# Bands and output projection of an encoder trunk: odd pairs' value products ahead of the scores, the last value splits in two steps, and the second half's normalising on VectorE

## The chip, the cores and the metric

The kernel runs on one core of a Trainium2 chip. The core has a matrix engine (TensorE, "PE" in the profile, with its weight loads listed apart as "PEld"), VectorE ("DVE"), ScalarE ("ACT"), GpSimd ("POOL") and a queue that issues most DMAs (SyncE, "SP"). Each engine works through its own instructions in order. The metric is the device time of one execution in microseconds (us); the median of some runs is compared.

## The reference

The reference is a trunk of two layers over 1024 tokens of width 1024, all in float32. Each layer computes

```python
h = rms_norm(x, g_attn[l]) * (1 + sc_a) + sh_a
proj = h @ w_in[l]
qa, ka, va, qb, kb, vb, qc, kc, vc = split_cols(proj, IN_SPLITS)
ya = neighborhood_attention(...)      # A: 4 heads, 2-D window with a relative bias
yb = sliding_window_attention(...)    # B: 6 heads on 2 key heads, |i-j| <= 128, sink logit
yc = axial_attention(...)             # C: 6 heads on 2 key heads, dense, rotary
ga, gb, gc = split_cols(g_group[l], GROUP_WIDTHS)
y = jnp.concatenate([rms_norm(ya, ga), rms_norm(yb, gb), rms_norm(yc, gc)], axis=-1)
x = x + gt_a * (y @ w_o[l])
h = rms_norm(x, g_ffn[l]) * (1 + sc_f) + sh_f
gate, up = split_cols(h @ w_gu[l], (FFN_HIDDEN, FFN_HIDDEN))
x = x + gt_f * ((jax.nn.silu(gate) * up) @ w_down[l])
```

A last RMS norm closes the trunk. What matters here: three groups of heads (widths 256, 384 and 384) give parts of `y`; each part is normalised over its own width, multiplied with a gain, and the whole goes through one output projection `w_o`.

## The kernel before, in words

**Layout.** Activations stand transposed: 128 features on the partitions, tokens along the free dimension. `y` has eight chunks of 128 features by 1024 tokens: chunks 0 and 1 are group A, 2 to 4 group B, 5 to 7 group C. Tokens are worked in two halves of 512 (`H`). To keep float32 accuracy on TensorE, an operand is split into a rounded high part and a low part (the rest), and a product is three matmuls: high x high, low x high, high x low (`mm3`, line 202).

**Attention as a stream of pairs.** Lines 1732 to 1744 write the work as a list of 64 pairs: six C heads, four A heads, six B heads, each with four pairs `p` = 0 to 3 of two query blocks (256 queries). The loop over turns `n` (line 1767) handles several pairs at once, each at another step. Pairs 0 to 23 are dense (C); pairs 24 to 63 are the bands (class `Band`, line 1560), whose queries see three key blocks each. In a turn of the bands (lines 1794 to 1814), for pair numbers around `n`, the steps are:

- `divide` of an older pair (VectorE reciprocal, then GpSimd scales the probabilities), `low` of pair n-1 (VectorE computes the low part of the transposed probabilities), `combine` of pair n-3 (VectorE adds the two halves of the value products into `y`; in the profile `y<-pv,cmb`);
- `scores` of pair n+4 (TensorE `sA` or `sB`, then VectorE adds the bias and takes the row's bound);
- `exps` of an older pair (ScalarE);
- `turn` of pair n: TensorE transposes the probabilities (`T`), ScalarE casts the middle blocks to the high part (`pt<-T`) and copies the edge blocks (`edge<-T`);
- `pv` of pair n-2: TensorE multiplies with the values into `pv`; then `fold` of the same pair: ScalarE copies one half of the partitions (`cmb<-pv`).

`fold` and `combine` do something only for odd pairs (line 1433 and 1442), because two pairs share one PSUM bank of 512 columns: the even pair opens a new `pv` tile in `products` (line 1413), the odd one fills its other half. The pool of these tiles has one bank (`bufs=4 - PS_T`, line 1361; `PS_T` is 3, the number of banks for `T`). So the products of an even pair wait until `combine` has read the bank for the pair before. Since pairs and turns have the same parity, even pairs are multiplied in even turns.

**What sets the order.** In the bands the instructions of TensorE, ScalarE and VectorE are pinned: `pin` (line 92) chains each to the one before it on its engine, so that these three run in the order of the program text. Instructions written while nothing is pinned are placed by a planner, which goes by data that is ready and by estimated costs, and can put them far ahead of their place in the text. That holds for what a turn does behind its `pin(..., False)` (line 1822): value splits, weight splits, output-projection rows, statistics.

**Norms.** When a group's pairs are done, `stats` (line 1865) sums squares over the partitions with one-column matmuls (`ps_st`) and takes the inverse root with a chain of small VectorE instructions (`inv_sqrt`; `isq` and `rstd` in the profile), all 1024 tokens at once. Eight turns after the group's end `norm_scale` (line 1684) follows: for each half, `spread` (line 449) makes four transposes that lay the 512 factors out over all partitions (`ps_r`), ScalarE copies them to `rb`, and one multiply for each chunk writes the normalised `y<-y,rb`. In the bands this is done for group C (three chunks) and A (two), both halves on GpSimd, one multiply a turn. Group B ends with the bands; it is normalised in the output projection, at `ki == 3` (line 1921), one half on VectorE and the other on GpSimd.

**Value splits.** `y_split` (line 1702) multiplies a chunk's half with the gain: ScalarE writes the high part, VectorE the low part. The first half's five normalised chunks (in the order `korder`: 5, 6, 7, 0, 1) go to a tile `yq`, which the profile calls `qk`: two are written in turns 55 and 59 (line 1837), three in the output projection at `ki == 0` (line 1916).

**Output projection.** Six of the eight output columns (`NK`) accumulate in PSUM over the chunks in the order `korder`, `ki` = 0 to 7; four of them (`NS`) start inside turns 61 to 64 (lines 1845 to 1848). The loop `for ki in range(5)` (line 1910) does the other columns and chunks, then columns 6 and 7, then `ki` = 5 to 7 with the split group B. The weights `w_o` come by DMA into two staging buffers and are split by ScalarE (`whi`) and VectorE (`wlo`). After that the second half is split for all chunks (line 1962) and projected.

Of the kernel before, what the change touches and what calls it, by code (L numbers as in the profile page):

```python
# [10 lines left out]
F32 = mybir.dt.float32  # L11
# [8 lines left out]
P = 128  # L20
D = 1024
S = 1024
KC = D // P
H = 512
# [61 lines left out]
def trunk(ctx: ExitStack, tc, A, C, out):  # L86
# [320 lines left out]
    def rstd_cols(ssqs, width, nt, sp_, psp, tag="mm", newton=False):  # L407

        ps = psp.tile([P, 512], F32, name="ps_st", tag=tag)
        for j in range(nt):  # L410
            for i, s in enumerate(ssqs):
                pe.matmul(
                    ps[:, j : j + 1],
                    s[:, j * P : (j + 1) * P],
                    ones,
                    start=(i == 0),
                    stop=(i == len(ssqs) - 1),
                )
        r = sp_.tile([P, 8], F32, name="rstd", tag="rstd", bufs=2)
        if newton:  # L420
            inv_sqrt(r[:, :nt], ps[:, :nt], width, sp_)
            return r
        act.activation(r[:, :nt], ps[:, :nt], AF.Sqrt, bias=epst, scale=1.0 / width)
        dve.reciprocal(r[:, :nt], r[:, :nt])
        return r
# [479 lines left out]
    for l in range(2):  # L905
# [775 lines left out]
            square(sq)  # L1681
            pool.tensor_tensor(out=ss[:, c], in0=ss[:, c], in1=sq, op=ALU.add)

        def norm_scale(chunks, r, psp, tag, engines):

            todo = []
            for half, eng in enumerate(engines):
                c = slice(half * H, (half + 1) * H)
                ps = spread(r, 4 * half, psp, tag=tag)
                rb = atp.tile([P, H], F32, name="rb", tag="rb", bufs=2)  # L1690
                act.copy(rb, ps)
                for n in chunks:
                    todo.append(
                        lambda eng=eng, n=n, c=c, rb=rb: eng.tensor_tensor(
                            out=y[:, n, c], in0=y[:, n, c], in1=rb, op=ALU.mult
                        )
                    )
            return todo

        korder = (5, 6, 7, 0, 1, 2, 3, 4)  # L1700

        def y_split(k, half, hi, lo):

            c = slice(half * H, (half + 1) * H)
            g = vec[:, 64 + k : 65 + k]
            act.activation(hi, y[:, k, c], AF.Copy, scale=g)
            dve.scalar_tensor_tensor(
                out=lo, in0=y[:, k, c], scalar=g, in1=f32(hi), op0=ALU.mult, op1=ALU.subtract
            )

# [44 lines left out]
            23: ((5, 6, 7), 384.0), 39: ((0, 1), 256.0), 63: ((2, 3, 4), 384.0),  # L1757
        }
        begins = {23: 0, 39: 24, 63: 40}
        later = {}  # L1760
        N = len(stream)
        pairs = {}
# [4 lines left out]
        for n in range(-AHEAD - 1, N + 3):  # L1767
# [26 lines left out]
            else:  # L1794
# [4 lines left out]
                if NC <= n - 3:  # L1799
                    pairs[n - 3].combine()  # L1800
                fresh = [pairs[m] for m in begin if m < made]
                for b in fresh:
                    b.scores()
                for b in scored:
                    b.exps()
                if n < N:
                    pairs[n].turn()
                if NC <= n - 2 < N:
                    pairs[n - 2].pv()
                    pairs[n - 2].fold()  # L1810
                elif n == NC:
                    for i in range(2):
                        pairs[n - 1].pv(i)
# [23 lines left out]
            if n in (55, 59):  # L1837
                ki = (n - 55) // 4
                y_split(korder[ki], 0, yq[:, ki, 0:H], yq[:, ki, H:S])
            if n in (59, 61):  # L1840
                w01.append(split_tile(wst.pop(0), 1, (atp, "pr", 6), dve))
            if n == 60:
# [9 lines left out]
            for end, (chunks, width) in norms.items():  # L1852
                if begins[end] <= m <= end and (m - begins[end]) % 8 == 7 and (n <= NC or m >= NC):
# [9 lines left out]
                    if m == end and end < N - 1:  # L1863

                        def stats(end=end, width=width, n=n, chunks=chunks):
                            r = rstd_cols([gss[end]], width, 8, atp, psT, tag="T", newton=True)

                            def scale():
                                todo = norm_scale(chunks, r, psT, "T", (pool, pool))
                                for i, what in enumerate(todo):  # L1870
                                    later.setdefault(n + 9 + i, []).append(what)

                            later.setdefault(n + 8, []).append(scale)

                        later.setdefault(n + 5, []).append(stats)
# [34 lines left out]
        for ki in range(5):  # L1910
            if ki < 2:
                o_rows(ki, w01[ki], range(NS, NK))
                w_ahead(3)
            else:
                o_rows(ki, w_next(), range(NK))
            if ki == 0:
                for i in range(2, 5):
                    y_split(korder[i], 0, yq[:, i, 0:H], yq[:, i, H:S])
            if ki == 2:
                r = rstd_cols([gss[N - 1]], norms[N - 1][1], 8, atp, psl, newton=True)  # L1920
            if ki == 3:
                for what in norm_scale(norms[N - 1][0], r, psl, "mm", (dve, pool)):
                    what()
                yb = [
                    atp.tile([P, 3, H], F32R, name="yb", tag="zA", bufs=2) for _ in range(2)
                ]
                for i in range(3):
                    y_split(2 + i, 0, yb[0][:, i, :], yb[1][:, i, :])
# [661 lines left out]
```

## Time and profile before

| what | value |
|---|---|
| median of 3 runs | 2369.87 us (2369.44 to 2372.74) |
| the profiled execution, its own time | 2368.57 us |
| its span, first to last instruction | 2366.8 us |
| granted TensorE clock, mean | 0.998 |
| busy: TensorE, VectorE, ScalarE, GpSimd | 2325.0, 1756.6, 1184.7, 775.7 us |
| bands of the first layer | about 364 to 464 us of the span |
| its output projection, first half | about 464 to 509 us |
| bands of the second layer | about 1521 to 1622 us |

How to read the lines in this document: an instruction is written as output `<-` inputs by the program's tile names, with buffer numbers left out, then partitions x elements and type. All lines carry "L49", the line of the helper that records every operation, so one goes by the tiles. In a listing in order of time the columns are start, duration (from the first start to the last end where equal neighbours are merged, `x` and their count) and the engine; in square brackets stands how long the engine had been idle and what ended that. In a list of waits the columns are the waiting engine and tile, what it waited for, the total in us, how many times, and the longest. Matmuls overlap, so the time that a group costs is read from its start to the next group's start.

### The profile page before, as it was taken

What the parts mean: (1) busy time and instruction counts of PE and PEld (TensorE: products, weight loads), DVE (VectorE), ACT (ScalarE), POOL (GpSimd) and SP (SyncE); (2) the same over time, 40 slices, a digit from 0 to 9 for tenths busy, and PEclk for the clock granted to TensorE, in tenths of its full rate; (3) what the DMA queues carried; (4) which work ended last, traced back from release to release, by engine and by line L of the source; (5) the groups of instructions that cost most, each with busy time, mean ns of one, the idle gap of its engine ahead of it and who ended that gap; (6) DMA issues with size and microseconds to landing.
All of it is one profiled execution on the core that took longest, in us unless ns stands there. A gap on an engine that the chain in (4) does not pass through costs nothing. (4 is left out here: it accounts for less than half of the span.)

```text
span 2366.8 us, 33472 instructions
## 1 busy us (share of the span) xinstructions
PE 2325.0 (98%) x11804; PEld 1959.9 (83%) x11804; DVE 1756.6 (74%) x2753; ACT 1184.7 (50%) x2261; POOL 775.7 (33%) x747
## 2 busy tenths in 40 slices
PE   9999999999999999999999999999999999999998
PEld 7888898888788888788888889988878888888886
DVE  6877998869867677595767789897796674537765
ACT  4423888845543333344633168896454434334443
POOL 1530447610344445100145124574005444430001
PEclk9999999999999999999999999999999999999999
DMA  8667416162434444775434861332634443239633
GB/s 280 182 207 227 127 27 192 44 217 94 138 130 165 156 138 151 217 245 175 155 100 133 247 186 28 92 103 94 218 98 132 154 150 103 98 106 299 209 120 112
DMA packets 307417, 358.02 MB, mean 151 GB/s; under 512 B 51996, under 2 KB 223868, under 8 KB 307248
## 3 DMA queue, kind: packets, MB, share of 16 engines
q1 hardware_dynamic: 290752, 346.26, 46.4%
q10 hardware_dynamic: 16128, 9.44, 1.5%
q8 instruction: 93, 1.52, 0.3%
q14 instruction: 76, 0.62, 0.1%
q0 software_dynamic: 368, 0.17, 0.0%
HBM read 270.84 MB, written 88.63 MB: 152 GB/s over the span
## 5 line engine op out<-in xcount | busy, mean ns | idle before, releaser
L49 PE MATMUL ps_d<-wpt 128*128 128x512 f32 x1848 | 423.8, 390 | 1.0 <-ACT wpt L49 0.7
L49 PEld LDWEIGHTS ps_d<-wpt 128*128 128x128 f32 x1848 | 345.7, 188 | 74.4 <-issue 3.0
L49 POOL TENSOR_SCALAR pr<-pr,rs 128x1024 f32<-128x1024 f32 (+2 forms) x248 | 190.3, 780 | 186.2 <-DVE rs L49 169.7
L49 POOL TENSOR_TENSOR sg<-sg,u 128x512 f32<-128x512 f32 x82 | 118.0, 1440 | 348.4 <-ACT sg L49 221.6
L49 PE MATMUL pv<-pt,vs 128*128 128x256 f32 x1088 | 173.9, 296 | 14.6 <-DVE y L49 13.3
L49 DVE TENSOR_TENSOR pt<-T,pt 128x512 fp32r<-128x512 f32 x272 | 177.4, 680 | 7.0 <-ACT pt L49 5.9
L49 ACT CAST wpt<-w 128x512 fp32r<-128x512 f32 x154 | 95.7, 621 | 173.5 <-PE ps_d L49 155.3
L49 DVE SCALAR_TENSOR_TENSOR acc<-wmt,condT,acc 128x512 f32<-128x512 f32 (+1 forms) x98 | 117.0, 1202 | 77.7 <-DMA wmt<-in_w_mod_dram 77.2
L49 ACT CAST pt<-T 128x512 fp32r<-128x512 f32 x272 | 151.5, 585 | 42.0 <-PE T L49 40.7
L49 ACT COPY u<-ps_w 128x512 f32<-128x512 f32 x128 | 75.1, 586 | 192.9 <-PE ps_w L49 192.9
L49 POOL TENSOR_TENSOR wpt<-ws,wpt 128x512 fp32r<-128x512 f32 x80 | 111.2, 1390 | 182.2 <-ACT wpt L49 137.2
L49 DVE TENSOR_TENSOR wpt<-w,wpt 128x512 fp32r<-128x512 f32 x154 | 108.9, 707 | 79.2 <-ACT wpt L49 76.9
L49 PEld LDWEIGHTS pv<-pt,vs 128*128 128x128 f32 x1088 | 141.0, 189 | 27.2 <-DVE y L49 25.2
L49 PE MATMUL T<-identr,pr 128*128 128x128 f32 x1176 | 160.1, 273 | 0.9 <-ACT edge L49 0.5
L49 PEld LDWEIGHTS T<-identr,pr 128*128 128x128 f32 x1176 | 137.7, 140 | 16.0 <-issue 1.4
L49 ACT CAST wpt<-ws 128x512 fp32r<-128x512 f32 x176 | 107.7, 622 | 52.9 <-issue 22.9
L49 DVE TENSOR_TENSOR wpt<-graw,wpt 128x512 fp32r<-128x512 f32 x154 | 109.8, 713 | 16.6 <-ACT wpt L49 16.4
L49 ACT CAST wpt<-graw 128x512 fp32r<-128x512 f32 x154 | 95.0, 617 | 52.7 <-DMA graw<-gpd 43.6
L49 DVE TENSOR_TENSOR wpt<-ws,wpt 128x512 fp32r<-128x512 f32 x96 | 82.7, 869 | 49.3 <-ACT wpt L49 49.1
L49 DVE TENSOR_TENSOR ws<-wr 128x512 f32<-128x512 f32 x88 | 81.2, 923 | 50.0 <-POOL wpt L49 46.6
L49 DVE TENSOR_REDUCE rs<-sC 128x1 f32<-128x1024 f32 x88 | 107.4, 1221 | 12.7 <-PE sC L49 11.4
L49 PE MATMUL ps_w<-ht3h,wpt 128*128 128x512 f32 x352 | 108.8, 390 | 2.4 <-ACT sg L49 2.4
(306 smaller groups left out, 5931.5 us busy)
## 6 DMA issues: line engine op xcount, KB each, us to landing
wr<-in_w_gu_dram SPq DMA_DIRECT2D x92, 512.0 KB, 4.2
gpd<-sg SPq DMA_DIRECT2D x154, 256.0 KB, 4.4
graw<-gpd SPq DMA_DIRECT2D x76, 512.0 KB, 3.5
w<-in_w_down_dram SPq DMA_DIRECT2D x110, 256.0 KB, 5.4
wmt<-in_w_mod_dram SPq DMA_DIRECT2D x48, 512.0 KB, 5.9
qk<-qkd SPq DMA_DIRECT2D x44, 512.0 KB, 7.2
wst<-in_w_o_dram SPq DMA_DIRECT2D x32, 512.0 KB, 4.4
wmt<-in_w_mod_dram SPq DMA_DIRECT2D x64, 256.0 KB, 3.9
```

Source lines behind the costliest of these rows:

```text
L49: ins = op(*args, **kwargs)
```

## The change

Three edits are made together.

1. In a turn of the bands, the value products `pv` of pair n-2 are issued ahead of the scores and the transposes if that pair is odd, and as before behind the transposes if it is even. `fold` stays behind the transposes in both cases.
2. `y_split` is taken apart: `y_high` issues ScalarE's high part and returns VectorE's low part as a function to be called later. The three splits that stood at `ki == 0` of the output projection are now issued in turns 62 to 64, the high part in one turn, the low part in the next (63 to 65), and both engines are pinned for them.
3. `norm_scale` takes a list of (half, engine). In the bands it is called for the first half alone, on GpSimd. The factors `r` of groups C and A are kept in a list `held`, and at `ki == 1` of the output projection the second half is spread and multiplied on VectorE. For this the tile `rstd` has three buffers instead of two where the chain of small instructions is used.

```diff
-        r = sp_.tile([P, 8], F32, name="rstd", tag="rstd", bufs=2)
+        r = sp_.tile([P, 8], F32, name="rstd", tag="rstd", bufs=3 if newton else 2)
...
-        def norm_scale(chunks, r, psp, tag, engines):
+        def norm_scale(chunks, r, psp, tag, halves):
 
             todo = []
-            for half, eng in enumerate(engines):
+            for half, eng in halves:
                 c = slice(half * H, (half + 1) * H)
                 ps = spread(r, 4 * half, psp, tag=tag)
                 rb = atp.tile([P, H], F32, name="rb", tag="rb", bufs=2)
...
-        def y_split(k, half, hi, lo):
+        def y_high(k, half, hi, lo):
 
             c = slice(half * H, (half + 1) * H)
             g = vec[:, 64 + k : 65 + k]
             act.activation(hi, y[:, k, c], AF.Copy, scale=g)
-            dve.scalar_tensor_tensor(
+            return lambda: dve.scalar_tensor_tensor(
                 out=lo, in0=y[:, k, c], scalar=g, in1=f32(hi), op0=ALU.mult, op1=ALU.subtract
             )
+
+        def y_split(k, half, hi, lo):
+            y_high(k, half, hi, lo)()
...
+        held, y_low = [], []
...
                 fresh = [pairs[m] for m in begin if m < made]
+                ready = pairs[n - 2] if NC <= n - 2 < N else None
+                if ready and ready.p % 2:
+                    ready.pv()
                 for b in fresh:
                     b.scores()
                 for b in scored:
                     b.exps()
                 if n < N:
                     pairs[n].turn()
-                if NC <= n - 2 < N:
-                    pairs[n - 2].pv()
-                    pairs[n - 2].fold()
+                if ready:
+                    if ready.p % 2 == 0:
+                        ready.pv()
+                    ready.fold()
                 elif n == NC:
...
+            if n >= 62:
+                pin((act, dve), True)
+                if y_low:
+                    y_low.pop()()
+                if n < 65:
+                    ki = n - 60
+                    y_low.append(y_high(korder[ki], 0, yq[:, ki, 0:H], yq[:, ki, H:S]))
+                pin((act, dve), False)
...
                             r = rstd_cols([gss[end]], width, 8, atp, psT, tag="T", newton=True)
 
+                            held.append((chunks, r))
+
                             def scale():
-                                todo = norm_scale(chunks, r, psT, "T", (pool, pool))
+                                todo = norm_scale(chunks, r, psT, "T", ((0, pool),))
...
-            if ki == 0:
-                for i in range(2, 5):
-                    y_split(korder[i], 0, yq[:, i, 0:H], yq[:, i, H:S])
+            if ki == 1:
+                for chunks, r in held:
+                    for what in norm_scale(chunks, r, psl, "mm", ((1, dve),)):
+                        what()
             if ki == 2:
                 r = rstd_cols([gss[N - 1]], norms[N - 1][1], 8, atp, psl, newton=True)
             if ki == 3:
-                for what in norm_scale(norms[N - 1][0], r, psl, "mm", (dve, pool)):
+                for what in norm_scale(norms[N - 1][0], r, psl, "mm", ((0, dve), (1, pool))):
                     what()
```

## The prediction

> **What bounds the kernel now.** I read the page first, then busy time by stretch, then the waits of the first layer's bands, and last the instructions in order of time in one head and in the stretch behind it.
>
> ```profile
> span 2366.8 us, 33472 instructions
> PE 2325.0 (98%) x11804; PEld 1959.9 (83%) x11804; DVE 1756.6 (74%) x2753; ACT 1184.7 (50%) x2261; POOL 775.7 (33%) x747
> ```
>
> TensorE is busy 98% of the span, so what can be won is mostly its idle 41.8 us, and whatever adds to it is lost. Stretches of the first layer (columns: length, then busy time and count of PE, PEld, DVE, ACT and POOL, granted clock, DMA):
>
> ```profile
> 394.99:453.60 58.61, 53.70 (x412) 50.63 (x412) 54.53 (x170) 55.90 (x158) 48.23 (x87) 1.00 0.21 62
> 453.60:464.44 10.84, 10.02 (x67) 8.15 (x66) 8.07 (x10) 7.64 (x18) 8.17 (x8) 1.00 0.30 101
> 464.44:489.00 24.56, 24.44 (x128) 20.34 (x127) 14.09 (x23) 10.85 (x15) 5.74 (x5) 1.00 0.40 128
> ```
>
> In the bands TensorE idles 4.9 of 58.6 us and ScalarE only 2.7. In the output projection TensorE idles 0.12 of 24.56: an instruction added to TensorE there costs its full time. The waits between 350 and 460 us:
>
> ```profile
> PEld pv L49 <- DVE y L49: 10.1, 15, 1.6
> PE pv L49 <- DVE y L49: 6.1, 10, 1.3
> ACT pt L49 <- PE T L49: 5.9, 11, 1.1
> ACT cmb L49 <- PE pv L49: 1.5, 3, 0.9
> DVE pr L49 <- POOL pr L49: 0.4, 1, 0.4
> ```
>
> TensorE's longest wait is the value products `pv` on the combine `y`. But ScalarE waits on TensorE's transposes `T` nearly as long, and that decides what the first edit does. Two pairs of turns, from all engines:
>
> ```profile
> 403.57 0.69 DVE L49 TENSOR_TENSOR y<-pv,cmb 64x512 f32<-64x512 f32 x1
> 404.32 0.74 PE L49 MATMUL pv<-pt,vs 128*128 128x256 f32 x4 [0.49 <-DVE y L49]
> 405.27 0.95 PE L49 MATMUL sB<-qk 128*128 128x384 f32 x4
> 406.06 0.82 PE L49 MATMUL T<-identr,pr 128*128 128x128 f32 x6
> 406.63 0.72 PE L49 MATMUL pv<-pt,vs 128*128 128x256 f32 x4
> 406.69 0.59 ACT L49 CAST pt<-T 128x512 fp32r<-128x512 f32 x1 [0.28 <-PE T L49]
> 407.18 0.38 ACT L49 COPY edge<-T 128x256 f32<-128x256 f32 x1
> 407.33 0.96 PE L49 MATMUL sB<-qk 128*128 128x384 f32 x4
> 407.67 0.58 ACT L49 COPY cmb<-pv 64x512 f32<-64x512 f32 x1
> 408.28 0.69 DVE L49 TENSOR_TENSOR y<-pv,cmb 64x512 f32<-64x512 f32 x1 [0.19 <-ACT cmb L49]
> 409.03 0.74 PE L49 MATMUL pv<-pt,vs 128*128 128x256 f32 x4
> 409.75 0.83 PE L49 MATMUL sB<-qk 128*128 128x384 f32 x4
> 410.42 0.71 PE L49 MATMUL T<-identr,pr 128*128 128x128 f32 x5
> 410.88 0.72 PE L49 MATMUL pv<-pt,vs 128*128 128x256 f32 x4
> 411.43 0.57 ACT L49 CAST pt<-T 128x512 fp32r<-128x512 f32 x1
> 411.80 0.83 PE L49 MATMUL sB<-qk 128*128 128x256 f32 x4
> 411.89 0.27 ACT L49 COPY edge<-T 128x128 f32<-128x128 f32 x1
> 412.19 0.58 ACT L49 COPY cmb<-pv 64x512 f32<-64x512 f32 x1
> 412.81 0.68 DVE L49 TENSOR_TENSOR y<-pv,cmb 64x512 f32<-64x512 f32 x1
> ```
>
> This is a closed loop. The one bank of `pv` is free when `y` has read it; then come the even pair's products (404.32), the next turn's scores `sB` (405.27), its transposes (406.06), ScalarE's cast of them (406.69), the edge copy, the fold `cmb` (407.67), and `y` again (408.28). From end of `y` to end of `y` it is 4.71 us here (404.26 to 408.97) and 4.52 in the second pair of turns (408.97 to 413.49).
>
> **The change, part by part.**
>
> *Odd pair's products first.* The odd pair's products (406.63 to 407.33, 0.70 us; 410.88 to 411.80, 0.92 us) move from behind the transposes of an odd turn to ahead of its scores, directly behind the even pair's. That puts them inside the loop, since TensorE works in order, and `cmb` stays behind the cast of the same turn's transposes. What was beside the loop is now on it. First pair of turns: the cast already waited for T, so it comes 0.70 later; against that `cmb` no longer waits for the products. It started 0.49 after the two-block edge copy, and after a one-block one 0.30 (411.89 to 412.19); the copies differ by 0.11, and as products now end before, I take 0.22 back. 0.70 - 0.22 = 0.48. Second pair: the cast starts 0.63 after the first transpose when it waits for it (406.06 to 406.69), so at 410.42 it was ready at 411.05 and ran at 411.43: slack 0.38; 0.92 - 0.38 = 0.54. Mean 0.51 us an odd turn; bounds: 0 if something covers it, 0.81 if no slack is left, and -0.22 if only the fold's gain stays. The wait it aims at does not go: `y` is no earlier, and the even products still wait for it, longer than before.
>
> A layer has 20 odd turns (27 to 65). I count nine at 0.51 (31, 35, 37, 39, 41, 43, 45, 55, 57): 4.6 us. Seven I cost at nothing. In 29 and 47 a norm's sixteen one-column products stand behind the turn, and TensorE's own sum up to them is unchanged; in 27 the bands are only filling; in 59 to 65 TensorE has output projection to do (10.02 of 10.84 us busy above). If that cover is gone, they are 7 x 0.51 = 3.6 us a layer more. Turns 33, 49, 51 and 53 mix with the other two edits.
>
> *Normalising and value splits out of the bands.* In order of time, turns 50 and 51:
>
> ```profile
> 430.50 0.73 ACT L49 ACTIVATE qk<-y,vecs 128x512 fp32r<-128x512 f32 x1
> 430.83 1.05 PE L49 MATMUL ps_r<-identr,rstd 128*128 128x128 f32 x8
> 431.72 1.06 ACT L49 COPY rb<-ps_r 128x512 f32<-128x512 f32 x2
> 432.13 0.71 PE L49 MATMUL T<-identr,pr 128*128 128x128 f32 x5
> 433.28 0.58 ACT L49 CAST pt<-T 128x512 fp32r<-128x512 f32 x1
> 433.52 1.45 DVE L49 SCALAR_TENSOR_TENSOR qk<-y,vecs,qk 128x512 fp32r<-128x512 f32 x1
> 435.50 0.67 DVE L49 TENSOR_TENSOR y<-pv,cmb 64x512 f32<-64x512 f32 x1
> ```
>
> The `qk<-y,vecs` are the value splits, which the planner had pulled up here; three of a layer's five now go to turns 62 to 65. Each norm's spread shrinks from eight transposes to four (0.40 us off TensorE), and one of two `rb` copies goes (0.48 off ScalarE). In turn 51 the loop gets 0.92 for the odd products and loses 0.40, so T is 0.52 later, cast ready at 433.28: as before. But VectorE's 1.45 us split no longer stands ahead of `y`: low part at 433.9, `cmb` ends 0.58 + 0.77 after the cast starts, `y` at 434.65 and not 435.50: -0.85 us. Turn 33 has the other norm's spread: 0.70 - 0.40 - 0.22, some 0.1. In 49 and 53 `y` waits for VectorE's splits more than for `cmb`: 0, bound 0.5 each. The four together: -0.75. So the bands cost 4.6 - 0.75 = 3.85 us a layer.
>
> Five `y<-y,rb` multiplies a layer leave GpSimd. It was no bound: the row `DVE pr <- POOL pr` shows all that VectorE waited for it, 0.4 us; I take 0.
>
> *Where they go.* No DMA is added or moved, so SP's queue keeps its order; GpSimd's gets five instructions shorter. The rows of the output projection:
>
> ```profile
> L49 DVE TENSOR_TENSOR y<-y,rb x3: 693/1787/1790, 485.3 to 487.6; 128x512 f32<-128x512 f32 x3
> 474.80 1.29 POOL L49 TENSOR_TENSOR gss<-gss,gsq 128x512 f32<-128x512 f32 x1 [3.84 <-ACT gsq L49]
> 479.59 0.17 DVE L49 TENSOR_SCALAR isq<-ps_st 128x8 f32<-128x8 f32 x1 [5.59 <-PE ps_st L49]
> 464.64 1.05 ACT L49 CAST whi<-wst 128x1024 fp32r<-128x1024 f32 x1 [2.70 <-DMA wst<-in_w_o_dram]
> ```
>
> TensorE: two spreads of four transposes, 8 for 1.05 us by the `ps_r` row, in a stretch with no idle time: +1.05 us a layer. VectorE: 5 x 0.69 = 3.5 us if GpSimd is quiet, 5 x 1.79 = 8.9 if it is not. They fit ahead of 479.59, where VectorE had stood 5.59 us; behind them waits the last norm's chain of small operations, and for that TensorE's `ps_r`. GpSimd has one 1.29 us sum there, so I take 3.5 to 4.8: hidden. The three splits, 3 x 0.73 on ScalarE and as much on VectorE, stand ahead of casts, folds and weight splits in turns 62 to 65; ScalarE's 2.70 us wait for a weight load hides them. If not, at most 3 x 0.73 = 2.2 us a layer. The third buffer of `rstd` lets the statistics live until used; nothing waits for it.
>
> For those multiplies the Trainium skill, page "SBUF — State Buffer", section "SBUF: two separate sides", has a rule: a VectorE instruction with two SBUF inputs and a GpSimd instruction that reads SBUF lock the shared ports for a whole instruction, and the loser is blocked. The trace agrees (0.69 us alone, 1.79 beside GpSimd). By it a multiply is slowed only while GpSimd runs, which gives the 4.8 us; if GpSimd ran throughout, it would be the third rival below.
>
> **Sum.** (3.85 + 1.05) x 2 layers = 9.8 us. The profiled execution took 2368.57 us (span 2366.8 and 1.8 around it); with 9.8 it is 2378.4. The median shown, 2369.87, lies 1.3 higher, so I forecast 2380 us: 0.4% slower. No change can be told from a difference within 0.2%, that is 4.7 us.
>
> **Rivals.**
> *The loop is not what limits* (faster). If the cast had slack for the odd products, `cmb` would gain 0.22 in one odd turn of each head and the relief of the bands would show. Then: 10 heads x 0.22 = 2.2, turn 51 at about 1.1 (the split's 1.45 less what `cmb` allows), 0.4 in turn 33, 0.4 in turn 53, less 1.05: 3.05 a layer, 6.1 together, 2364 us. For it: TensorE's 6.1 us of waits on `y`. Against: the cast's own waits for T (5.9 us, 11 times). It decides where the slack exceeds 0.70 to 0.92; the rows show -0.28 and 0.38.
> *The edits cancel* (same). If only half of the nine turns pay, 2.3 - 0.75 + 1.05 = 2.6 a layer, 2375 us; if none does, 0.3 a layer, 2370.5 us. For it: ScalarE and VectorE were near full in the bands, and the planner may place freed work better. Moving splits which had been hoisted anyway may also just shift them.
> *The multiplies delay the last norm* (slower still). At 8.9 us on VectorE 3.3 us do not fit into 5.59; the `ps_r` transposes come late and TensorE stands: 2 x 3.3 = 6.6 more, 2387 us. Against: GpSimd's single sum there.
> *Every odd turn pays*: 20 x 0.51 + 0.3 = 10.5 a layer with the spreads, 2391 us.
>
> **How the numbers follow.** The loop as costed 0.50; every odd turn 0.10; late norm 0.08; cancelling 0.15 (0.05 of it above the 0.2% bound); loop not limiting 0.17. Slower: 0.50 + 0.10 + 0.08 + 0.05 = 0.73; same 0.10 and a share 0.02 of the fifth: 0.12; faster 0.15. The range 2366 to 2391 leaves out most of the fifth case and the far end of the second. The likeliest case alone: 2375 to 2387.
>
> **What would show it.** Right: in odd turns two groups of `pv` stand directly behind one another and then `sB` and `T`; ScalarE's wait for T grows from 5.9 us by several us, the wait of `pv` for `y` does not shrink, undisturbed heads last about 10.2 us and not 9.2 to 9.3; eight `ps_r` transposes stand among the `ps_o` near 475 us; five `y<-y,rb` of about 0.7 us on VectorE there. Wrong: heads of 9.2 us or less, `y` earlier against the cast, or a wait of `ps_r` for `rstd` of over 1 us.

## The result and the profile after

| | us |
|---|---|
| before, median of 6 runs | 2370.29 (2369.44 to 2372.74) |
| after, median of 6 runs | 2384.61 (2381.91 to 2386.81) |
| ratio after / before | 1.0059, 95% interval 1.0049 to 1.0069 |
| profiled executions, before and after | 2368.57 and 2384.08 |

The change costs 14.3 us by the medians and 15.5 us between the two profiled executions. The forecast was 2380 in a range of 2366 to 2391, slower with 0.73.

The first lines of the page of the changed kernel, and then its windows for the stretches shown of before (the bands up to the first row of the output projection, the last turns, and the 24.56 us behind them):

```profile
span 2382.3 us, 33439 instructions
PE 2329.4 (98%) x11804; PEld 1961.5 (82%) x11804; DVE 1763.7 (74%) x2763; ACT 1186.7 (50%) x2261; POOL 762.9 (32%) x737
```

```profile
397.69:460.42 62.73, 53.82 (x410) 50.57 (x411) 51.62 (x165) 54.48 (x155) 40.45 (x81) 1.00 0.17 50
460.42:471.12 10.70, 10.38 (x68) 8.35 (x66) 7.22 (x12) 8.19 (x18) 8.03 (x8) 1.00 0.29 100
471.12:495.68 24.56, 22.88 (x123) 18.65 (x122) 16.43 (x30) 11.71 (x18) 3.08 (x2) 1.00 0.41 129
```

TensorE's share of the span is the same 98%, and its work too (11804 instructions). But the bands' stretch, with TensorE busy for the same 53.7 to 53.8 us, is 62.73 us long and not 58.61: TensorE idles 8.9 us there instead of 4.9. And in the output projection's 24.56 us, where it idled 0.12 us, it now idles 1.68. The waits between 350 and 460 us of the changed kernel:

```profile
PEld pv L49 <- DVE y L49: 16.6, 18, 1.5
ACT pt L49 <- PE T L49: 13.0, 19, 1.1
PE pv L49 <- DVE y L49: 12.1, 15, 1.2
```

The products' wait for `y` doubled (6.1 to 12.1), and ScalarE's wait for the transposes more than doubled (5.9 to 13.0): the engines now stand waiting for each other around the loop. Two pairs of turns of the changed kernel, all engines in order of time:

```profile
402.26 0.68 DVE L49 TENSOR_TENSOR y<-pv,cmb 64x512 f32<-64x512 f32 x1
403.00 0.73 PE L49 MATMUL pv<-pt,vs 128*128 128x256 f32 x4 [0.69 <-DVE y L49]
403.70 0.72 PE L49 MATMUL pv<-pt,vs 128*128 128x256 f32 x4
404.63 0.83 PE L49 MATMUL sB<-qk 128*128 128x384 f32 x4
405.30 0.71 PE L49 MATMUL T<-identr,pr 128*128 128x128 f32 x5
405.94 0.59 ACT L49 CAST pt<-T 128x512 fp32r<-128x512 f32 x1 [0.41 <-PE T L49]
406.71 0.58 ACT L49 COPY cmb<-pv 64x512 f32<-64x512 f32 x1
407.32 0.69 DVE L49 TENSOR_TENSOR y<-pv,cmb 64x512 f32<-64x512 f32 x1
408.07 0.74 PE L49 MATMUL pv<-pt,vs 128*128 128x256 f32 x4 [0.93 <-DVE y L49]
409.01 0.72 PE L49 MATMUL pv<-pt,vs 128*128 128x256 f32 x4
409.71 0.96 PE L49 MATMUL sB<-qk 128*128 128x384 f32 x4
410.50 0.82 PE L49 MATMUL T<-identr,pr 128*128 128x128 f32 x6
411.14 0.59 ACT L49 CAST pt<-T 128x512 fp32r<-128x512 f32 x1 [0.89 <-PE T L49]
411.62 0.38 ACT L49 COPY edge<-T 128x256 f32<-128x256 f32 x1
412.02 0.58 ACT L49 COPY cmb<-pv 64x512 f32<-64x512 f32 x1
412.63 0.69 DVE L49 TENSOR_TENSOR y<-pv,cmb 64x512 f32<-64x512 f32 x1
```

An even pair's products and the next odd pair's stand directly behind one another, then scores, then transposes; and TensorE stands still ahead of each even group. From end of `y` to end of `y` it is 5.07 us (402.94 to 408.01) and 5.31 (to 413.32). The pair with the two-block edge copy is the one of 5.31, which took 4.71 before; the other took 4.52. The first two heads of group B, which no norm disturbs, last 10.37 and 10.40 us (start of one head's first scores to the next one's, from 395.39) where they lasted 9.20 and 9.35 (from 393.25).

Rows of the output projection of the changed kernel:

```profile
473.67 0.68 DVE L49 TENSOR_TENSOR pt<-T,pt 128x512 fp32r<-128x512 f32 x1
473.78 1.33 ACT L49 ACTIVATE qk<-y,vecs 128x512 fp32r<-128x512 f32 x2
474.27 0.74 DVE L49 SCALAR_TENSOR_TENSOR qk<-y,vecs,qk 128x512 fp32r<-128x512 f32 x1
475.07 0.74 PE L49 MATMUL ps_o<-qk,whi 128*128 128x512 f32 x2 [1.40 <-DVE qk L49]
484.14 1.03 PE L49 MATMUL ps_r<-identr,rstd 128*128 128x128 f32 x8
485.45 3.10 DVE L49 TENSOR_TENSOR y<-y,rb 128x512 f32<-128x512 f32 x5 [3.56 <-ACT rb L49]
488.58 0.17 DVE L49 TENSOR_SCALAR isq<-ps_st 128x8 f32<-128x8 f32 x1
```

The eight `ps_r` cost 1.03 us, and the five multiplies take 3.10 us: five of 0.6 to 0.7, as costed with GpSimd quiet, behind 3.56 us in which VectorE stood idle. New is the wait of `ps_o` at 475.07. The pinned split's low part (474.27) stands on VectorE behind the low part of a turn's transposes, which stands behind casts on ScalarE; the projection's matmuls need it and TensorE stands 1.40 us. Over both layers this wait comes to 2.6 us, the longest 1.4. The rest of the 1.68 us of idle time is a wait of 0.28 us for the copies `rb`, which the kernel before does not have either.

Where the 15.5 us are, by stretch from one landmark to the next, after minus before, from the start times of the instructions named:

| stretch | first layer | second layer |
|---|---|---|
| first scores of group A to the last `sB` | 92.50 to 98.94: +6.44 | 101.37 to 107.66: +6.29 |
| last `sB` to the first `ps_o<-yb` | 41.81 to 43.26: +1.45 | 42.10 to 43.06: +0.96 |

That is 15.1 of the 15.5 us. Cut at the last even product group ahead of the projection instead (457.06 before, 463.76 after), the first layer's 7.9 us are 5.7 in the bands and 2.2 behind them.

### The profile page after: what moved, and what is told of

Same layout as the page of the kernel before. It is cut to its first block, busy times and chain, and to the rows that moved or that the text cites. A ratio compares the mean times of both kernels' runs of the same rounds, so it can differ in the third digit from the quotient of the medians.

```text
span 2382.3 us, 33439 instructions
## 1 busy us (share of the span) xinstructions
PE 2329.4 (98%) x11804; PEld 1961.5 (82%) x11804; DVE 1763.7 (74%) x2763; ACT 1186.7 (50%) x2261; POOL 762.9 (32%) x737
## 5 line engine op out<-in xcount | busy, mean ns | idle before, releaser
L49 PE MATMUL ps_w<-h22h,wpt 128*128 128x512 f32 x352 | 109.0, 391 | 1.8 <-ACT sg L49 1.0
```

What stands on the lines that cost most here:

```text
L49: ins = op(*args, **kwargs)
```

## The experiments

Two theories. *The loop*: the odd pair's products became part of a closed loop through the one bank of `pv`, and each odd turn pays for them; the other two edits hardly count. *The placement*: it is the moved splits and the moved normalising (planner, VectorE, the extra wait in the output projection) that cost, and the order of the products is hidden. Ratios below stand to the kernel before on the same chip, and so do the differences in us in the text; medians of runs on different chips are not compared with each other. "Heads" are the first two of group B in the first layer, as above.

| run | median us | ratio, 95% interval | heads, us |
|---|---|---|---|
| before (in the five comparisons) | 2370.29, 2370.11, 2372.50, 2372.59, 2373.05 | | 9.20, 9.35 |
| after | 2384.61 | 1.0049 to 1.0069 | 10.37, 10.40 |
| edit 1 alone | 2386.56 | 1.0055 to 1.0083 | 10.40, 10.38 |
| edits 2 and 3 | 2369.73 | 0.9990 to 1.0007 | 9.22, 9.23 |
| edit 2 alone | 2369.64 | 0.9986 to 1.0004 | 9.20, 9.34 |
| edit 3 alone | 2374.01 | 1.0006 to 1.0023 | 9.20, 9.24 |
| half the odd products first | 2381.71 | 1.0028 to 1.0056 | 9.73, 9.73 |
| edit 1, fold ahead of the cast | 2387.08 | 1.0051 to 1.0076 | 10.00, 10.27 |
| edit 1, fold and combine early | 2376.96 | 1.0013 to 1.0033 | 8.68, 10.45 |
| all edits, fold and combine early | 2371.74 | 0.9991 to 1.0009 | 8.62, 9.01 |
| before, fold ahead of the edge copy | 2375.16 | 1.0003 to 1.0021 | 9.31, 9.46 |
| the same with edit 2 | 2369.07 | 0.9981 to 0.9999 | 9.30, 9.46 |
| edits 1 and 2, fold and combine early | 2371.13 | 0.9989 to 1.0007 | 8.68, 10.44 |
| after with two banks for `pv` | 2383.40 | 1.0032 to 1.0061 | 9.12, 9.14 |

### One edit at a time

The first edit alone (`odd_first`), on the kernel before:

```diff
+                ready = pairs[n - 2] if NC <= n - 2 < N else None
+                if ready and ready.p % 2:
+                    ready.pv()
                 for b in fresh:
                     b.scores()
...
-                if NC <= n - 2 < N:
-                    pairs[n - 2].pv()
-                    pairs[n - 2].fold()
+                if ready:
+                    if ready.p % 2 == 0:
+                        ready.pv()
+                    ready.fold()
```

> The kernel before with the first edit alone: odd pairs' products ahead of the scores. Theory 1 (the loop): the products lengthen the closed loop y, even products, odd products, scores, transposes, cast, fold, y. Undisturbed heads last 10.2 to 10.5 us instead of 9.2 to 9.3, and since neither the spreads nor the splits have left the bands, the whole costs 10 to 14 us: about 2382 us. Theory 2 (placement): most of the 14.3 us comes from what was put among the output projection's matmuls; then this kernel costs under 5 us.

The changed kernel with that edit undone (`rest_only`), the second edit alone (`splits_only`) and the third alone (`norm_only`):

> The changed kernel with the first edit undone: splits in two steps and the second half's normalising in the output projection. Theory 1: heads of 9.2 to 9.3 us as before; the relief of the bands (about 1 us a layer) against 1.05 us of spreads and about 1.4 us of waiting for a split's low part in the output projection a layer: 0 to +3 us in all. Theory 2: +7 us or more.

> The kernel before with the second edit alone: three value splits in two steps in turns 62 to 65. Theory 1: the head around the first layer's 424 to 436 us gets shorter by about 1 us, TensorE waits 1 to 1.5 us a layer for a split's low part near 475 us: -1 to +2 us in all. If the wait for the low part belongs to this edit, it is here and not in the third edit's kernel.

> The kernel before with the third edit alone: second half's normalising on VectorE in the output projection. Theory 1: TensorE has 1.05 us a layer more there, the bands 0.4 to 0.9 us a layer less: 0 to +2 us in all, and no wait of ps_o for a split's low part over 0.5 us.

Edit 1 alone costs 16.4 us, no less than the whole change (the intervals overlap), and gives the heads of the changed kernel. The other two together cost nothing that can be measured (-0.4 us), so the placement theory falls. The runs do not quite add: the splits alone are even (-0.5), the normalising alone costs 3.9, and both together -0.4. Three expectations missed in part: edit 1 alone cost more than the 10 to 14 us expected, edit 3 alone more than 0 to 2, and the wait for a split's low part, 1 to 1.5 us a layer, is not there with edit 2 alone, which has a single one of 0.2 us.

That edit 1 alone costs no less than the three edits has a likely cause in the trace. Rows of it, in order of time:

```profile
440.02 0.71 PE L49 MATMUL T<-identr,pr 128*128 128x128 f32 x5
440.63 1.29 POOL L49 TENSOR_TENSOR y<-y,rb 128x512 f32<-128x512 f32 x1
441.95 0.72 ACT L49 ACTIVATE qk<-y,vecs 128x512 fp32r<-128x512 f32 x1 [1.81 <-POOL y L49]
442.58 0.56 ACT L49 CAST pt<-T 128x512 fp32r<-128x512 f32 x1
443.18 0.69 DVE L49 TENSOR_TENSOR pt<-T,pt 128x512 fp32r<-128x512 f32 x1 [1.85 <-ACT pt L49]
443.37 0.33 PE L49 MATMUL T<-identr,pr 128*128 128x128 f32 x1 [1.61 <-ACT edge L49]
```

The planner pulled a value split into the bands, ahead of the chunk it reads: ScalarE stands 1.81 us for GpSimd's `y<-y,rb`, with the cast of finished transposes queued behind it, and VectorE (1.85) and TensorE (1.61) stand for ScalarE. The head there lasts 12.28 us, where the same head of the changed kernel lasts 10.38. In the second layer the same wait stands at 1605.74, with 1.94 us. Neither the kernel before nor the changed one, where three of the five splits are pinned to later turns, has this wait. A second likely cause is in the section on the hardware.

Where do edits 2 and 3 leave the time that they free? With both (`rest_only`) the last scores start 90.23 us after the first scores of group A, against 92.50 before; in the second layer 99.83 against 101.37. But from there to the first `ps_o<-yb` it is 44.01 in both layers, against 41.81 and 42.10 (in the first layer 449.21 to 493.22, before 451.47 to 493.28).

So the relief of the bands is real, some 2 us a layer, and is given back between the last scores and group B's rows of the same layer's output projection. In the first layer half of that is work, the spreads' 1.03 us, and half is idle time: TensorE stands 1.99 us in this stretch instead of 0.94, most of it in products that wait for `y` (1.5 instead of 0.5), in the last turns, where the pinned splits stand on ScalarE and VectorE; with edit 2 alone that wait is 1.5 too.

### A dose of the suspected cause

Half of the odd pair's products (the first of the two groups, about 0.46 us) ahead of the scores, the other behind the transposes as before (`half_first`):

```diff
-            def pv(self):
+            def pv(self, parts=range(2)):
...
-                for part in range(2):
+                for part in parts:
                     self.products(movs, part)
...
+                if ready and ready.p % 2:
+                    ready.pv((0,))
                 for b in fresh:
                     b.scores()
...
+                    ready.pv((1,) if ready.p % 2 else (0, 1))
+                    ready.fold()
```

> The kernel before, with the odd pairs' products cut in two: the first four or so matmuls of a pair (0.46 us) ahead of the scores, the rest behind the transposes as before. Theory 1 (the loop with a slack): the cast of transposes has 0.38 us of slack in one odd turn of each two and none in the other, so 0.46 us on the loop cost 0.46 + 0.08 = 0.5 us a head of four turns, against 1.1 for the whole product: heads of 9.7 to 9.9 us, and 4 to 8 us in all. Theory 2 (the place in the turn counts, not the length): the same as the whole product moved, 14 to 17 us.

Heads of 9.73 and 9.73: 0.53 and 0.38 more than before, where the whole products gave 1.20 and 1.03. Half the dose, a little under half the cost in each head, as expected; the total (+9.2) is over the 4 to 8 us expected and somewhat over half of edit 1's 16.4, and this run also has the split that waits for GpSimd (1.38 us at 437.51) and two stretches of half clock (below).

### Can the loop be shortened on ScalarE?

Edit 1 with the odd pair's fold `cmb` ahead of the cast (`fold_early`), and then also with its combine `y` in the same turn, behind the scores' bias sums (`fold_combine`); the last also in the changed kernel (`all_fold_combine`) and without edit 3 (`splits_fold_combine`):

```diff
                 for b in scored:
                     b.exps()
+                if ready and ready.p % 2:
+                    ready.fold()
+                    ready.combine()
...
-                if NC <= n - 3:
-                    pairs[n - 3].combine()
```

(`fold_early` is without the `combine` line, and keeps the combine where it was.)

> The kernel before with the first edit, and with the odd pair's fold on ScalarE ahead of the turn's cast instead of behind it. Theory 1: no relief, since on VectorE the combine still stands behind the low part of the same turn's transposes, so that the loop only changes its last link: heads of 10.2 to 10.4 us, 2381 to 2387 us. Theory 3 (the fold's place behind the cast is what closes the loop): heads near 9.2 us, 2368 to 2373 us.

> The kernel before with the first edit, the odd pair's fold ahead of the turn's cast, and its combine in the same turn behind the scores' bias sums, so that neither stands behind transposes. Theory 1: the loop is opened, the wait of pv for y goes, and ScalarE sets the pace: heads of 9.0 to 9.2 us, 2364 to 2370 us. Theory 2 (the products are dear by their place whatever follows them): heads over 10 us, over 2380 us.

> The changed kernel with the same opening of the loop: fold ahead of the cast, combine behind the scores of the same turn. Theory 1: as the kernel without the first edit, or better by what the wait for y gives back: 2363 to 2370 us, with heads of 9.0 to 9.2 us. Theory 2: near the changed kernel's 2384.6 us.

> The first and the second edit, with the odd pair's fold ahead of the cast and its combine in the same turn; the normalising stays as before (both halves in the bands on GpSimd). With all three edits this order gave 2371.7, with the first alone 2377.0; the third edit alone cost 3.9. If costs add, 2367 to 2369 here. If it was the third edit that relieved the bands (one spread and one copy less in turns 33 and 51), it stays at 2375 to 2377, with heads of 11 around the second norm; if it was the second, about 2371.

The fold alone brings little, as the loop theory expected: heads of 10.00 and 10.27, and a total of +14.6 us, not clearly less than edit 1's 16.4. VectorE's combine still stands behind the low part of the turn's transposes, which waits for the cast, and so for TensorE's transposes: the loop closes through another engine. With fold and combine both ahead, `y` no longer needs the turn's transposes, and the loop is open. In the changed kernel heads fall to 8.62 and 9.01, below before, and most of the wait goes; from the waits of the changed kernel with fold and combine early, 350 to 460 us:

```profile
ACT pt L49 <- PE T L49: 4.5, 7, 0.9
PE pv L49 <- DVE y L49: 2.1, 4, 0.8
```

The products' wait for `y` is 2.1 us where the changed kernel had 12.1, and the total is that of before (ratio 1.0000): the 14.3 us are gone, with the odd products still ahead of the scores. With edit 1 alone (`fold_combine`) the same order misses its expectation of 2364 to 2370: of 16.4 us it leaves 4.5, and the second head stays at 10.45. So edit 1 costs through the loop and not by the place of the products as such. The fall below before that was expected (2363 to 2370) does not come: the last scores come 90.63 us after the first ones of group A, 1.9 earlier than before, and the projection gives it back (43.34 us to `ps_o<-yb` against 41.81), as with edits 2 and 3 alone. Without edit 3 (`splits_fold_combine`) it is as much (ratio 0.9998), so "costs add", 2367 to 2369, did not come out. The total is the one expected if the second edit had relieved the bands (about 2371), with the long head around the second norm (11.28) that was expected if the third had. Its first five heads of group B in the first layer are within 0.02 of those of `fold_combine`. Of the 7.9 us between the two profiled executions, 3.4 are half clock (below), and 1.4 lie in the sixth head of that layer, up to the last scores.

The second head is 10.45 in these two kernels and 9.01 with all three edits, and between `splits_fold_combine` and `all_fold_combine` the third edit is the only difference. Rows of `fold_combine` in that head:

```profile
404.19 1.26 POOL L49 TENSOR_TENSOR y<-y,rb 128x512 f32<-128x512 f32 x1
404.25 0.48 DVE L49 CUSTOM_DVE_ANT_0 pr<-sB,bz,sinkc 128x256 f32<-128x256 f32 x1 [0.58 <-POOL pr L49]
404.78 0.69 DVE L49 TENSOR_TENSOR y<-pv,cmb 64x512 f32<-64x512 f32 x1
405.53 0.74 PE L49 MATMUL pv<-pt,vs 128*128 128x256 f32 x4 [0.54 <-DVE y L49]
```

The sixth multiply of the first norm stands on GpSimd here, which is busy 8.54 of the head's 10.45 us. VectorE waits 0.58 us for GpSimd's `pr`, and the combine and the even products stand behind that. With all three edits GpSimd has three multiplies fewer, is busy 4.88 of 9.01 us, and no wait for it is listed in the head. So, with the loop open, GpSimd seems to bound this head, though it was no bound in the kernel before; the chain is read from these rows and was not tested apart.

The kernel before, with the fold between the cast and the edge copy in odd turns (`fold_mid`), and the same on top of edit 2 (`splits_mid`):

```diff
                 act.copy(hi, T)
                 e = self.e = atp.tile([P, 2, P], F32, name="edge", tag="edge", bufs=3)
-                act.copy(e[:, 0 : len(edges)], E[:, 0 : len(edges)])
...
+                return lambda: act.copy(e[:, 0 : len(edges)], E[:, 0 : len(edges)])
...
                     pairs[n - 2].pv()
                     pairs[n - 2].fold()
+                    if (n - 2) % 2 and n < N:
+                        edge()
```

> The kernel before with one move on ScalarE alone: in an odd turn the fold cmb stands between the cast of the transposes and the edge copy, not behind the edge copy. TensorE's and VectorE's orders are unchanged. Loop theory: the loop's part cast, edge, cmb, y becomes cast, cmb, y. In the first pair of turns cmb can then start when the products end (about 407.4 instead of 407.67) and y when VectorE's low part is through (408.09 + a gap, instead of 408.28): 0.1 to 0.2 us less. In the second pair the low part ends at 412.72 and y stands at 412.81 already: 0.05 less. So heads of 9.0 to 9.1 instead of 9.20 and 9.35, 1 to 2 us a layer, 2366 to 2369 against 2370. Rival, the loop is not limiting: heads unchanged, 2370. If the edge copy was needed early, heads get longer.

> The same move of the fold on top of the second edit alone (three value splits in turns 62 to 65). The second edit alone gave no measurable difference. Loop theory: both add, 2365 to 2369. If the time saved in the bands is only spent waiting in the output projection, 2369 to 2370.

A miss: heads of 9.31 and 9.46, longer by 0.11 and not shorter, and the total 2.6 us up. ScalarE and VectorE rows of `fold_mid`:

```profile
407.52 0.59 ACT L49 CAST pt<-T 128x512 fp32r<-128x512 f32 x1
408.49 0.58 ACT L49 COPY cmb<-pv 64x512 f32<-64x512 f32 x1 [0.39 <-PE pv L49]
409.10 0.69 DVE L49 TENSOR_TENSOR y<-pv,cmb 64x512 f32<-64x512 f32 x1 [0.19 <-ACT cmb L49]
```

Directly behind the cast the fold waits 0.39 us for the odd products, which stand behind the transposes on TensorE. In the order before, the edge copy filled just that time; here it runs behind the fold and takes time of its own. So there was no slack between cast and `y` to be had in that order. With edit 2 on top (expected 2365 to 2370) the total is 2369.07, 0.1% under before on its chip (0.9981 to 0.9999): the lowest ratio of all, but too near to no change to call it a gain.

### Taking the loop away

The changed kernel with two banks for `pv` and two for the transposes (`two_banks`):

```diff
-PS_T = 3
+PS_T = 2
```

> The changed kernel with all three edits and one constant changed: two PSUM banks for the products pv and two for the transposes T, instead of one and three. The even pair's products then need not wait for the combine y of the pair before them. Loop theory: the wait of pv for y (22.6 us over both layers, and as much on the weight loads) is gone and undisturbed heads fall from 10.4 to what TensorE's own work takes, 8.6 to 9.0 as with fold and combine moved, unless the third bank of T was needed. A turn uses two of them; the next turn's T needs the bank that low has read, and by the rows of the changed kernel low ends 1.5 us ahead of that, so the bands should not need the third. The dense pairs also use T and may lose by it; no row prices that. If they lose nothing, 2370 to 2374; if they lose, the heads of the bands decide, not the total. Rival (the odd pair's products cost as such, not through the bank): heads stay at 10.4.

No instruction of the bands now waits for `y` on TensorE, and heads last 9.12 and 9.14 us (from 399.63 to 408.75 and 417.89): not quite the 8.6 to 9.0 expected, and far from the rival's 10.4. What stands now among the waits of 350 to 460 us, where `pv` on `y` stands no more:

```profile
ACT pt L49 <- PE T L49: 9.7, 19, 1.9
PE T L49 <- DVE pt L49: 3.3, 4, 1.3
```

The same order of instructions that cost 1.1 us a head costs nothing in them once the second bank is there. That is the loop theory shown by its own resource. The total gains less: it stands 10.4 us above before on its chip, where the changed kernel stands 14.3 above, and the intervals overlap. In the profiled executions, 1.1 us apart, the gain in one place is lost in another: from the first scores of group A to `ps_o<-yb` the layers are 3.9 and 5.6 us shorter than in the changed kernel, but the stretches ahead of these, with the dense pairs, are 2.7 and 6.3 us longer (362.68 against 359.97, and 1019.19 from `ps_o<-yb` to the second layer's first scores of A against 1012.88). That the dense pairs miss the third bank of `T` is the likely reason and was not tested; in the longer of these two stretches it is TensorE's busy time that grows (1007.94 to 1013.29 us), its idle time by 1.0 us. In the bands, where the expectation was that the third bank is not needed, the second row above shows a new wait, of the transposes for VectorE's low part, which has to read the bank first.

## Why the prediction was right

The sign and the cause were right: the loop through the bank of `pv`, read from the rows of before, is what costs. The size came out low, 9.8 us forecast against 14.3, and two terms were too small for it. Step by step:

- *The loop of a pair of turns.* Forecast 4.71 + 0.48 = 5.19 and 4.52 + 0.54 = 5.06; measured 5.31 and 5.07. The second, from ScalarE's slack of 0.38, is met. In the first the 0.22 taken back for `cmb` was too much: it starts 0.40 after the two-block edge copy (411.62 to 412.02), not 0.27, so it took back only 0.09.
- *Heads of about 10.2*, ScalarE's wait for `T` up by several us, the products' wait for `y` not shrinking: 10.37 and 10.40, 13.0 us, 12.1 us. Right.
- *Nine turns at 0.51, seven at nothing.* This term was mis-sized, and it is most of what is missing. From one head's even products to the next head's, first layer, after minus before against the forecast: +1.26 (0.51), +0.29 (0.61), +1.05 (1.02), +1.17 (1.02), +1.37 (0.51), -0.93 (-0.85), +0.78 (0.51), +0.56 (0.51); in sum 5.55 against 3.84. In the third and fourth, where only the loop works, the forecast holds within 0.15. The fifth holds turn 47, which I costed at nothing since TensorE's own sum up to the sixteen one-column products stays as it was. That was the wrong end of the loop: VectorE's queue decides there, by the rows below. Before, the turn's low part ran ahead of the norm's first instruction `isq`, which waits for those products, and `y` stood directly behind that; after, the planner has `isq` ahead of the low part, so that the low part waits too and `y` comes 0.98 behind `isq` and not 0.20. The first has the planner's doing in it as well: the first norm's `ps_r` were put ahead of the products, and TensorE waited 0.50 us for `rstd` there (at 386.59).

Around turn 47, the kernel before and then the changed one:

```profile
421.27 0.69 DVE L49 TENSOR_TENSOR pt<-T,pt 128x512 fp32r<-128x512 f32 x1 [0.18 <-ACT pt L49]
422.97 0.17 DVE L49 TENSOR_SCALAR isq<-ps_st 128x8 f32<-128x8 f32 x1 [1.00 <-PE ps_st L49]
423.17 0.69 DVE L49 TENSOR_TENSOR y<-pv,cmb 64x512 f32<-64x512 f32 x1
```

```profile
428.49 0.17 DVE L49 TENSOR_SCALAR isq<-ps_st 128x8 f32<-128x8 f32 x1 [1.20 <-PE ps_st L49]
428.65 0.67 DVE L49 TENSOR_TENSOR pt<-T,pt 128x512 fp32r<-128x512 f32 x1
429.47 0.69 DVE L49 TENSOR_TENSOR y<-pv,cmb 64x512 f32<-64x512 f32 x1
430.22 0.74 PE L49 MATMUL pv<-pt,vs 128*128 128x256 f32 x4 [0.53 <-DVE y L49]
```

- *Turn 51 gains 0.85 from the split moved away.* Measured -0.93 for the head that holds it. It is the only one of these eight that gets shorter.
- *Eight spreads at 1.05 with no idle time to hide in.* Measured 1.03 for the eight; right, but for the 0.28 us that TensorE then waits for their copies `rb`.
- *The moved splits are hidden.* Wrong in part: I looked for their cover on ScalarE (the wait for a weight load, now 1.53 us) and named VectorE's share without asking what stands ahead of the low part there. The new wait of the projection for it is 2.6 us in both layers together, inside the bound of 2.2 a layer. With the spreads it makes most of the 2.2 us behind the bands, where 1.05 was forecast. It takes the first edit too: with edit 2 alone, and with edits 2 and 3, this wait is 0.2 us, and with all three and the loop open there is none.
- *The multiplies on VectorE are hidden*, 3.5 to 4.8 us: 3.10. They end just ahead of the last norm's `isq` (485.45 + 3.10, and 488.58). TensorE's first matmul behind the norm's sums `ps_st` starts 0.48 us ahead of `isq` (488.10), where it was 0.17 in the kernel before (479.42 and 479.59), so they delay the norm by some 0.3 us, and TensorE has no wait for it. The rival "the multiplies delay the last norm" did not come; GpSimd had one sum there.
- *The rivals.* "The loop is not what limits" needed the cast to have slack; undoing edit 1 showed the reverse. "The edits cancel" describes edits 2 and 3 well: they relieve the bands by 2 us a layer and cost it again behind them, with no difference left. "Every odd turn pays" comes nearest of the rivals, since turns costed at nothing did pay; but its 10.5 us a layer is more than the 7.9 and 7.25 measured from the first scores of group A to the first `ps_o<-yb`.

In sum: 3.85 a layer for the bands was 5.7, and 1.05 for the projection was 2.2, in the first layer; 9.8 became 15.5 us between the profiled executions. Both errors go the same way, so none hides another. By the medians of its own comparison the change lies 4.6 us above the forecast, and within the likeliest case's own range of 2375 to 2387.

## What to carry to other kernels

Where several in-order engines hand a single buffer around, add up the loop from its release back to its release, with each engine's queue order; work that is moved into that loop costs its time less the slack that the rows show (here 0.92 less 0.38), whatever the busy shares look like, and what took the cost away here was to break the loop (a second buffer, or a combine that does not need the next transposes). Before costing a turn at nothing, look at what the last member of the loop stands behind on its own engine, not only at the engine that has the cover. And relief in one stage is worth only what the next stage does not take back: here 2 us a layer came out of the bands and went into the turns and the projection behind them. Opening one loop can also hand the bound to an engine that had room before, as GpSimd's rows suggest.

## What was unexpected of the hardware

TensorE's granted clock falls to half inside the bands, in some of the profiled executions and not in others. Windows of edit 1 alone, first a stretch of the first layer, then of the second (the granted clock is the third number from the end):

```profile
430.00:432.00 2.00, 2.00 (x11) 2.00 (x12) 2.00 (x10) 1.42 (x5) 0.65 (x2) 0.51 0.00 0
432.00:434.00 2.00, 2.00 (x11) 1.97 (x11) 0.91 (x2) 1.07 (x2) 1.03 (x2) 0.63 0.00 0
```

```profile
1606.00:1608.00 2.00, 0.33 (x1) 0.14 (x1) 0.95 (x2) 1.98 (x5) 2.00 (x5) 0.91 0.34 98
1608.00:1610.00 2.00, 1.52 (x7) 1.52 (x8) 1.99 (x7) 1.98 (x9) 2.00 (x2) 0.50 0.00 0
```

Product groups of four take 1.22 us there instead of 0.74. The first comes behind sixteen one-column products (1.84 us) and a stand of 0.52, the second behind the stands of 1.62 and 1.00 us that the late split causes. Counted over windows of 2 us, one minus the clock times the length, the bands lose 5.1 us this way with edit 1 alone, 5.1 with fold and combine early on top of it, 3.4 with half the products first, 3.4 with two banks, 1.7 each in four others, and nothing in the kernel before, in the changed kernel and in the four that are left. (The changed kernel loses 1.7 us at 32 us of its span, far from the bands; the kernel before loses nothing there.) With edit 1 alone, 16.4 less 5.1 is 11.3, but that is read from one profiled execution of each kernel, so how much of a median it makes is not shown. The same sixteen products stand in the profiles of the kernel before and of the changed one without a loss. Nor is it a matter of the kernel alone: of 27 executions of the kernel before on one chip, the six with a mean granted clock of 0.995 took 2373.97 us in the median, the five with 0.998 took 2370.22.

The Trainium skill, "TensorE: Matmul & The Clock Gate", section "Part 1: The HAM clock gate", says that the array falls to half rate after at least one idle window of about 3.4 us, and that this window runs freely. The trace agrees on the half rate (0.50 and 0.51), and 1.7 us lost at half rate is a slow stretch of 3.4 us. It does not show an idle window of that length: ahead of the slow stretches in the bands TensorE's longest stand was 2.41 us (with edit 2 alone, for a DMA) and 1.9 us or less in all others. So shorter stands, with or without one-column products beside them, went ahead of the slow stretches here; what of that counted as idle is not shown.
